# A gated delta layer: smaller tiles in the chunk's inverse, gate weights kept split in memory, and loads asked for at other points

## The chip, the cores and the metric

The kernel runs on one core of a Trainium2 chip. A core has a tensor engine (PE), whose weight loads the profile lists apart as PEld, a vector engine (DVE), a scalar engine (ACT), a general engine (POOL) and an engine that mostly starts transfers (SP); DMA queues move data between the device memory and the on-chip memory. Each engine works through its own row of instructions in order and waits on semaphores where it needs another's result. The metric is the device time of one execution in microseconds (us); less is better. All times below are of the kernel before the change.

## The reference, cut to what matters

One inference step of two layers over 2048 prompt tokens and 32 sample tokens, all in 32-bit floats. The first layer is a gated DeltaNet, the second an attention over a sliding window. The change is in the first layer and in its gate projection and output projection:

```python
proj = x @ w_in                                   # q, k, v, gate z, decays, betas
qkv, new_buf = causal_conv(proj[..., :CONV_DIM], conv_buf, conv_w)
z = proj[..., CONV_DIM:CONV_DIM + A_VW]
...
lower = where(strict, einsum('nbhik,nbhjk->nbhij', k * beta, k) * decay, 0)   # 64 x 64 per chunk and head
tmat = lower + eye(c)
u = triangular_solve(tmat, v * beta)              # needs the inverse of tmat
w = triangular_solve(tmat, k * beta * exp(gcum))
intra = einsum('nbhik,nbhjk->nbhij', q, k) * decay
def step(s, xs):                                  # one chunk after the other
    v_new = ui - wi @ s
    o = qd @ s + ai @ v_new
    s = s * gl + kd.T @ v_new
...
o = o * rsqrt(mean(o * o) + eps) * norm_w * silu(z)
x = layer_norm(alpha * x + o @ w_out)
```

## The kernel before, in words

Every large product is made of three: a 32-bit operand is split into a high part and a rest, and high times high, high times rest and rest times high are summed. Weights come from memory raw (`fetch_weights`), ACT rounds them to `w_hi` (L53), and POOL subtracts that for `w_lo` (L54); `project` then issues 24 products L77, L78 and L79 for a block of 416 tokens, in four steps of six.

The work goes through these stages, one after the other:

1. `P1.qkv`, to about 586 us: the projections of q, k and v, with the convolution on DVE and ACT.
2. The gate's first pass, `P1.z` over the token blocks 0, 1 and 2 for 8 heads, to about 704 us. Each head's 128 columns of weights are fetched and split. A block ends in a tanh on ACT (`zth`, L310), two operations on DVE (L311, L312) and a store by SP (L313). Beside it `Ahead.inverses` makes the small inverses of the first two chunks (`c0`, the 32 sample tokens, and `c1`): a product `g` (L536), a decay `E` (add L516 on DVE, exp L522 on ACT), `npr` = g times E, and a chain of 31 small steps on DVE (L559, L562).
3. The gate's second pass over blocks 3 and 4 for the same 8 heads, which fetches and splits the same weights again. It is not run by itself: `first`, a `Filler`, hands out its steps of six products at fixed places of the next stage.
4. `Delta.run`, the loop over 17 chunks (`i` = 0 is the sample chunk, then 16 of 128 tokens) from about 761 us, one turn taking some 24 to 29 us. The order of its instructions on PE, DVE and ACT is the order in which the code issues them (`manual_schedule`); SP's and POOL's order is left to a scheduler. One turn works on four chunks at once: it inverts the triangular matrix of chunk i+1, makes `g` and `E` of later ones, carries the state `Sp` of chunk i on, and scales its output. The inverse of a chunk and 8 heads has two levels. POOL (and DVE for the last rows) does 31 steps of elimination on 32 x 32 blocks (`chain`); DVE transposes the result into `tcp` (L628, L629). Then `invert` puts the blocks together by products, with the results copied out between them:
   - y1 = the 32 x 32 blocks below the diagonal (products L652, copied out by ACT at L654),
   - `tp` (L658) and `up` (L665), 64 x 64 products with `u32`, which ACT has made of `tcp` by two scaled copies (L634); ACT copies `tp` at L660 and half of `up` at L666, DVE the other half at L667,
   - y2 (L671), copied by ACT at L672, and the last product u2 (L676), copied by ACT at L677 into `u`, with which `vp` (L697) is made.
   Between them stand products that have nothing to do with the inverse: `gq` (L601), `tr` (L572, copied by ACT as `kd`, L575), `vtr` (L586), `op` (L711), and the filler's six at a time.
   The rest of a turn: `npr` (L537) on DVE, `nb` (L541) on ACT, DVE's transpose of it into `L` (L546), the chain's last steps and `tcp` again; `otr` (L771) and `z` (L772) bring out the output.
5. `O1`, the output projection with its layer norm (L1008 to L1013), whose 16 weight tiles `wo` (L955) and two tables are loaded from turn 12 on (`side`), and whose first token tile is fetched and split (`g_hi`, L994, `g_lo`, L995) when its products are due.
6. The second layer, from about 1250 us.

Of the kernel before, what the change touches and what calls it, by code (L numbers as in the profile page):

```python
# [19 lines left out]
D = 1024  # L20
# [142 lines left out]
class P1:  # L163
# [49 lines left out]
    def qkv(self):  # L213
# [32 lines left out]
        for i in range(24):  # L246
# [8 lines left out]
            due += 224 / 22 if i >= 2 else 0  # L255
# [43 lines left out]
    def z(self, blocks, pool, tags, ps, sub, w, wait=False):  # L299

        nc = self.nc
        for h in range(8):
            self.fetched = fetch_weights(nc, self.wp, self.I["w_in"][25 + h]) if h < 7 else None
            self.next, self.sub = None, sub
            for b in blocks:
# [8 lines left out]
                if not wait or b == blocks[-1]:  # L314
                    self.split()
            w = self.next

    def split(self):
        if self.fetched is not None:
            self.next = split_fetched(self.nc, self.wp, self.fetched, self.sub)  # L320
            self.fetched = None

    def first_gate(self, sub):
        return split_weights(self.nc, self.wp, self.I["w_in"][24], sub)
# [123 lines left out]
class Delta:  # L448
# [5 lines left out]
    def __init__(self, tc, es, I, O, T, G):  # L454
# [13 lines left out]
        self.u32 = one.tile([128, 8, 64], F32, tag="u32", name="u32")  # L468
        self.sides = one.tile([128, 2], F32, tag="sides", name="sides")
        for b in range(4):  # L470
            for c in range(2):
                nc.gpsimd.memset(self.sides[32 * b:32 * b + 32, c:c + 1], float(b % 2 == c))
        self.u = one.tile([128, 8, 128], F32, tag="u", name="u")
        nc.gpsimd.memset(self.u[:], 0.0)
        self.y1 = one.tile([128, 8, 64], F32, tag="y1", name="y1")
        nc.gpsimd.memset(self.y1[:], 0.0)
        for hv in (slice(0, 64), slice(64, 128)):
            nc.gpsimd.tensor_copy(self.y1[hv], G["ident"][hv, hv].unsqueeze(1).to_broadcast([64, 8, 64]))
# [142 lines left out]
    def spread(self, ch):  # L621
# [3 lines left out]
        sml = self.sml  # L625
        both = sml.tile([128, 2, 8, 32], F32, tag="ta", name="tcp")
        ch.tcf, ucp = both[:, 0], both[:, 1]
        V.transpose(ch.tcf[:n].rearrange("q p (c d) -> q c d p", d=4), ch.Tt[:n].rearrange("q i c -> q c i"))  # L628
        V.transpose(ucp[:n], ch.tcf[:n])  # L629
        if n == 32:  # L630
            V.tensor_copy(self.u[:32, :, :32], ucp[:32])
            return
        for c in range(2):
            nc.scalar.activation(self.u32[:, :, 32 * c:32 * c + 32], ucp[:], AF.Copy, scale=self.sides[:, c:c + 1])  # L634

    def invert(self, ch):

        nc, V = self.nc, self.nc.vector
        if ch.n == 32:
            return  # L640
        u, sml = self.u, self.sml
        u32, npr = self.u32, ch.npr
        halves = (slice(0, 64), slice(64, 128))

        def new(pool):
# [1225 lines left out]
```

## Time and profile before

| | us |
|---|---|
| median of 3 runs | 2263.8 (2253.85 to 2264.89) |
| the profiled execution | 2252.59 |
| its span | 2250.8 |
| stage 1, `P1.qkv` | to about 586 |
| stages 2 and 3 up to the loop | 586 to about 761 |
| loop `Delta.run` | about 761 to 1190 |
| rest of `O1` | to about 1250 |
| second layer | to the end |

The span runs from the first to the last instruction of the trace; the execution's own time is 1.8 us longer. All times in the text count from the span's start. The trace gives each instruction a start and a duration. A bracket such as `[3.28 <-ACT zth L310]` says that the engine stood idle for 3.28 us before it, and that the last thing it waited for was the tile `zth` that ACT writes at line 310. "PEclk" is the clock granted to PE as a share of the full one.

### The profile page before, as it was taken

The numbers are of one execution on the slowest core, as the hardware profiler recorded it, in microseconds if no ns is written. First come the engines' busy times: TensorE is split into PE (matmuls) and PEld (weight loads), VectorE is DVE, ScalarE is ACT, GpSimd is POOL, SyncE is SP. The second block draws the span as 40 slices with busy tenths as digits, with TensorE's granted clock in tenths as the row PEclk, the third lists the DMA queues.
The fourth block names the chain that finished last, engine by engine and source line by source line (L and its number), as shares of the span: only waits on it lengthen the run. The fifth ranks groups of instructions, "written<-read, shape, count | busy, mean of one in ns | idle before, by whom it ended". The sixth has DMA issues, their size and how long they took to land. (4 is left out here: it accounts for less than half of the span.)

```text
span 2250.8 us, 37045 instructions
## 1 busy us (share of the span) xinstructions
PE 2152.2 (96%) x13370; PEld 1959.0 (87%) x13370; DVE 1470.4 (65%) x2701; ACT 902.7 (40%) x2331; POOL 740.9 (33%) x1193
## 2 busy tenths in 40 slices
PE   8999999999999999999889999899989998999997
PEld 6899999999998889988777787899989986888775
DVE  4798777876484577777655665545844566556662
ACT  4555555444332466656552211311311135444441
POOL 1213111251112387777661210000000024656563
PEclk9999999999999899999999999999999999999999
DMA  7656656567734334435724874888788896233321
GB/s 285 211 185 194 193 179 197 183 193 235 235 117 130 113 117 138 148 114 171 277 75 157 285 224 148 284 279 290 249 297 291 266 286 183 85 104 94 85 80 43
DMA packets 344919, 417.40 MB, mean 185 GB/s; under 512 B 77968, under 2 KB 275696, under 8 KB 344720
## 3 DMA queue, kind: packets, MB, share of 16 engines
q1 hardware_dynamic: 312432, 314.41, 44.1%
q10 hardware_dynamic: 32304, 100.62, 13.4%
q8 instruction: 106, 1.74, 0.3%
q14 instruction: 77, 0.63, 0.1%
HBM read 265.26 MB, written 150.05 MB: 185 GB/s over the span
## 5 line engine op out<-in xcount | busy, mean ns | idle before, releaser
L77 PE MATMUL ps<-act_hi,w_hi 128*128 128x416 f32 x1280 | 459.3, 359 | 6.4 <-ACT R L297 4.3
L79 PE MATMUL ps<-act_hi,w_lo 128*128 128x416 f32 x1280 | 451.7, 354 | 5.2 <-POOL w_lo L54 5.2
L78 PE MATMUL ps<-act_lo,w_hi 128*128 128x416 f32 x1280 | 451.8, 353 | 0.0
L77 PEld LDWEIGHTS ps<-act_hi,w_hi 128*128 128x128 f32 x1280 | 242.4, 189 | 11.2 <-ACT R L297 4.6
L79 PEld LDWEIGHTS ps<-act_hi,w_lo 128*128 128x128 f32 x1280 | 242.7, 190 | 9.7 <-POOL w_lo L54 6.3
L78 PEld LDWEIGHTS ps<-act_lo,w_hi 128*128 128x128 f32 x1280 | 243.2, 190 | 2.7
L54 POOL TENSOR_TENSOR w_lo<-w_raw,w_hi 128x1024 fp32r<-128x1024 f32 x40 | 101.5, 2537 | 381.5 <-ACT w_hi L53 374.9
L1232 PE MATMUL ps<-xs_h,w 128*128 128x416 f32 x560 | 199.4, 356 | 10.9 <-DVE ra L1289 6.9
L1233 PE MATMUL ps<-xs_l,w 128*128 128x416 f32 x560 | 199.9, 357 | 2.9 <-DVE xs_l L1135 2.9
L1234 PE MATMUL ps<-xs_h,w 128*128 128x416 f32 x560 | 198.2, 354 | 0.0
L266 DVE SCALAR_TENSOR_TENSOR y<-R,convw,y 128x2083 f32<-128x2083 f32 x72 | 171.2, 2379 | 24.5 <-ACT y L264 24.4
L559 POOL TENSOR_TENSOR tm<-L,Tt 128x60 f32<-128x60 f32 (+19 forms) x375 | 132.1, 352 | 86.3 <-DVE tm L559 34.1
L562 POOL TENSOR_TENSOR Tt<-Tt,tm 128x60 f32<-128x60 f32 (+19 forms) x375 | 143.4, 382 | 28.5
L1573 POOL TENSOR_TENSOR P<-P,sm 128x384 f32<-128x384 f32 (+2 forms) x128 | 101.0, 810 | 122.5 <-DVE sm L1452 59.1
L1427 POOL MEMSET vd<- 64x768 f32 (+2 forms) x10 | 7.8, 779 | 395.9 <-DVE ra L1289 395.6
L1448 ACT ACTIVATE P<-S,nm 128x192 f32<-128x192 f32 (+2 forms) x260 | 104.8, 419 | 61.4 <-DVE nm L1441 48.9
L1232 PEld LDWEIGHTS ps<-xs_h,w 128*128 128x128 f32 x560 | 106.3, 190 | 13.8 <-DVE ra L1289 7.6
L1289 DVE SCALAR_TENSOR_TENSOR ra<-ps,u 128x416 f32<-128x416 f32 x60 | 35.4, 590 | 122.0 <-PE ps L1234 121.2
L1008 PE MATMUL po<-wo,g_hi 128*128 128x512 f32 (+1 forms) x272 | 110.5, 406 | 3.0 <-DVE r L1013 1.8
L1010 PE MATMUL po<-wo,g_lo 128*128 128x512 f32 (+1 forms) x272 | 107.5, 395 | 4.5 <-DVE g_lo L995 4.5
L1233 PEld LDWEIGHTS ps<-xs_l,w 128*128 128x128 f32 x560 | 106.1, 189 | 5.5 <-DVE xs_l L1135 4.2
L1234 PEld LDWEIGHTS ps<-xs_h,w 128*128 128x128 f32 x560 | 106.9, 191 | 1.2
(292 smaller groups left out, 4808.7 us busy)
## 6 DMA issues: line engine op xcount, KB each, us to landing
w<-s_w ACTq DMA_DIRECT2D x180, 512.0 KB
s_w<-pre_hl SPq DMA_DIRECT2D x160, 256.0 KB
w_raw<-in_w_in SPq DMA_DIRECT2D x40, 512.0 KB
s_wo<-pre_hl SPq DMA_DIRECT2D x64, 256.0 KB
wo<-s_wo SPq DMA_DIRECT2D x32, 512.0 KB
gb<-s_gcum SPq DMA_DIRECT2D x34, 256.0 KB
k<-s_k SPq DMA_DIRECT2D x34, 256.0 KB
s_z<-z SPq DMA_DIRECT2D x40, 208.0 KB
```

The lines of the kernel that those rows point to most:

```text
L77: nc.tensor.matmul(ps, hi[:, k, :], xh[:, k, :], start=(k == 0), stop=False)
L78: nc.tensor.matmul(ps, hi[:, k, :], xl[:, k, :], start=False, stop=False)
L79: nc.tensor.matmul(ps, lo[:, k, :], xh[:, k, :], start=False, stop=(k == KC - 1))
L266: nc.vector.scalar_tensor_tensor(out=y[:], in0=R[:, j:j + W], scalar=self.convw[:, i, j:j + 1], in1=y[:], op0=ALU.mult, op1=ALU.add)
L559: P.tensor_tensor(out=tm[:n, i0 - k:, :w], in0=L[:n, i0:, j:j + 1].to_broadcast(sh), in1=Tt[:n, j:j + 1, :w].to_broadcast(sh), op=ALU.mult)
L562: P.tensor_tensor(out=Tt[:n, i0:, :w], in0=Tt[:n, i0:, :w], in1=tm[:n, i0 - k:, :w], op=ALU.subtract)
L1008: nc.tensor.matmul(ps[:n], ghi[:, k, :n], w[0][k][:, cs], start=(k == 0), stop=False)
L1010: nc.tensor.matmul(ps[:n], glo[:, k, :n], w[0][k][:, cs], start=False, stop=(k == KC - 1))
L1232: nc.tensor.matmul(ps, w[:, 0, k], xh[:], start=first and k == 0, stop=False, skip_group_check=True)
L1233: nc.tensor.matmul(ps, w[:, 0, k], xl[:], start=False, stop=False, skip_group_check=True)
L1234: nc.tensor.matmul(ps, w[:, 1, k], xh[:], start=False, stop=last and k == 3, skip_group_check=True)
L1448: nc.scalar.activation(P[u], src, AF.Exp, bias=nm[:, u:u + 1], scale=1.0, accum_out=sm[:, u:u + 1])
```

## The change

The gate's first pass stores each head's split weights in a new scratch in memory (`wz`, 8 x 2 x 512 KB, by SP), and the second pass reads them back, asked for by ACT's queue, so that L53 and L54 aren't done a second time:

```diff
+    def split_gate(self, sub):
+        w = split_weights(self.nc, self.wp, self.I["w_in"][24], sub)
+        for h in range(8):
+            raw = fetch_weights(self.nc, self.wp, self.I["w_in"][25 + h]) if h < 7 else None
+            yield w
+            for t, d in zip(w, self.T["wz"][h]):
+                self.nc.sync.dma_start(d, t[:].rearrange("p k c -> p (k c)").bitcast(F32))
+            w = split_fetched(self.nc, self.wp, raw, sub) if h < 7 else None
+            yield
+    def kept_gate(self):
+        def load(h):
+            w = [self.wp.tile([128, KC, 128], F32R, tag=t, name=t) for t in ("w_hi", "w_lo")]
+            for t, d in zip(w, self.T["wz"][h]):
+                self.nc.scalar.dma_start(t[:].rearrange("p k c -> p (k c)").bitcast(F32), d)
+            return w
+        w = load(0)
+        yield
+        for h in range(8):
+            ahead = load(h + 1) if h < 7 else None
+            yield w
+            yield
+            w = ahead
```

The inverses made ahead are now issued step by step between steps of the gate's first pass, in PE's order by hand:

```diff
-    Ahead(tc, mid, left, I, O, T, G).inverses(chunks[:2])
-    drain(p1.z((0, 1, 2), zp, ("zth", "z"), p1.ps, nc.gpsimd, p1.first_gate(nc.gpsimd)))
-    w = p1.first_gate(nc.gpsimd)
+    zs = p1.z((0, 1, 2), zp, ("zth", "z"), p1.ps, p1.split_gate(nc.gpsimd))
+    ahead = Ahead(tc, mid, left, I, O, T, G).inverses(chunks[:2])
+    with tc.manual_schedule(engines={mybir.EngineType.PE}):
+        for n in (18, 18, 6, 6, 12, 12):
+            next(ahead)
+            drain(itertools.islice(zs, n))
+        drain(ahead)
+        drain(zs)
+    kept = p1.kept_gate()
+    next(kept)
```

PE's order at that place, before: `g` of the sample chunk stands behind the first block's products (each row is an instruction or a run of alike ones; `act_hi_127` and `act_hi_153` are the blocks 0 and 1).

```order
L78 MATMUL ps<-act_lo_128,w_hi 128x416
L79 MATMUL ps<-act_hi_127,w_lo 128x416
L536 MATMUL g<-k 32x32 x8
L77 MATMUL ps<-act_hi_153,w_hi 128x416
L78 MATMUL ps<-act_lo_154,w_hi 128x416
```

And after: the first half of it stands behind 36 steps, 216 products, of which the last are of block 2 (`act_hi_164`), and the other half six steps further on.

```order
L78 MATMUL ps<-act_lo_165,w_hi 128x416
L79 MATMUL ps<-act_hi_164,w_lo 128x416
L550 MATMUL g<-k 32x32 x4
L77 MATMUL ps<-act_hi_128,w_hi 128x416
L78 MATMUL ps<-act_lo_129,w_hi 128x416
```

So `g` has moved from behind 24 products to behind 216.

In `invert`, `up` is made of 32 x 32 products straight from `tcp` and y1, y2 and u2 are given out in pairs of heads to two halves of the array, and the diagonal blocks are copied:

```diff
-        tp = new(self.pa)
-        for p in range(8):
-            nc.tensor.matmul(tp[:64, p, :], u32[:64, p, :], y1[:64, p, :], start=True, stop=True)
-        ta = sml.tile([128, 8, 64], F32, tag="ta", name="ta")
-        nc.scalar.copy(ta[:64], tp[:64])
+        for b in (0, 1):
+            bs = slice(32 * b, 32 * b + 32)
+            nc.scalar.copy(ta[bs, :, bs], tcf[bs])
         yield
         up = new(self.pb)
-            for hv in halves:
-                nc.tensor.matmul(up[hv, p, :], y1[hv, p, :], u32[hv, p, :], start=True, stop=True)
-        nc.scalar.copy(u[0:64, :, 0:64], up[0:64])
-        V.tensor_copy(u[64:128, :, 64:128], up[64:128])
+            for s, t in pairs:
+                nc.tensor.matmul(up[s, p, 0:32], y1[t, p, :], ucp[t, p, :], start=True, stop=True)
+            nc.tensor.matmul(up[t0, p, 0:32], ucp[t0, p, :], y1[t0, p, :], start=True, stop=True)
+        nc.scalar.copy(ta[t0, :, s0], up[t0, :, 0:32])
+        for s, t in pairs:
+            V.tensor_copy(u[s, :, t], up[s, :, 0:32])
+        V.tensor_copy(self.ub[0:32, :, 32:64], up[64:96, 4:8, 0:32])
+        V.tensor_copy(self.ub[0:32, :, 0:32], ucp[64:96, 4:8])
+        V.tensor_copy(self.ub[32:64, :, 32:64], ucp[96:128, 4:8])
         yield
...
+            for q, dst in ((p, high), (p + 4, low)):
+                nc.tensor.matmul(y2p[dst, q, :], npr[:64, q, 64:128], ta[:64, q, :], start=True, stop=True)
+        nc.scalar.copy(ta[high, 0:4], y2p[high, 0:4])
+        nc.scalar.copy(self.yb[:], y2p[low, 4:8])
+        for b in (2, 3, 0, 1):
+            bs = slice(32 * b, 32 * b + 32)
+            nc.scalar.copy(u[bs, :, bs], ucp[bs])
...
+            nc.tensor.matmul(u2p[low, p, :], ta[high, p, :], u[high, p, high], start=True, stop=True)
+            nc.tensor.matmul(u2q[low, p, :], self.yb[:, p, :], self.ub[:, p, :], start=True, stop=True)
+        nc.scalar.mul(u[low, 0:4, high], u2p[low, 0:4], -1.0)
+        nc.scalar.mul(u[low, 4:8, high], u2q[low, 0:4], -1.0)
```

ACT's order in one turn with filler work, before, from the inverse's first copy to the last exp (`bps` is the product's result, whichever it is; `zth` is the filler's tanh):

```order
L634 ACTIVATE u_6398<-tcp,sides 128x8x32 x2
L654 ACTIVATE y_6410<-bps 32x8x32 x2
L660 COPY ta<-bps 64x512
L575 ACTIVATE kd<-tr,t_ekd 128x128 x4
L666 COPY u<-bps 64x8x64
L610 ACTIVATE gb<-gb 128x512 x2
L672 COPY ta<-bps 64x512
L575 ACTIVATE kd<-tr,t_ekd 128x128 x4
L522 ACTIVATE E<-E,t_ngc 128x128 x4
L310 ACTIVATE zth<-ps 128x416
L677 ACTIVATE u<-bps 64x8x64
L522 ACTIVATE E<-E,t_ngc 128x128 x4
```

The same after; `zth` and the second four of `E` follow the last row.

```order
L662 ACTIVATE y_6423<-bps 32x256 x2
L665 COPY ta<-tcp 32x8x32 x2
L673 COPY ta<-bps 32x8x32
L589 ACTIVATE kd<-tr,t_ekd 128x128 x4
L685 COPY ta<-bps 64x256
L686 COPY yb<-bps 64x256
L689 COPY u<-tcp 32x8x32 x4
L624 ACTIVATE gb<-gb 128x512 x2
L695 ACTIVATE u<-bps 64x4x64
L696 ACTIVATE u<-bps 64x4x64
L589 ACTIVATE kd<-tr,t_ekd 128x128 x4
L536 ACTIVATE E<-E,t_ngc 128x128 x4
```

The copies of u2, one behind `zth` before, are two ahead of the second `kd` now, and four copies of diagonal blocks (L689) have come in ahead of `gb`.

The weights `wo` of `O1` are asked for by ACT's queue, one at each call of `side()`, which comes four times in a turn from turn 11 on; the tables at its twelfth step; and `O1`'s first token tile is fetched at turn 13 and split at turn 14:

```diff
-            if i > 11:
-                side(True)
+            side()
...
+            side()
+            if i in (13, 14):
+                second.step()
...
-            nc.sync.dma_start(w[:, k, s].bitcast(F32), src[k, :, s])
+            queue.dma_start(w[:, k, s].bitcast(F32), src[k, :, s])
...
-        got = self.on.split(self.fetch(*tiles[0]), tiles[0][2])
+        got = self.fetch(*tiles[0])
+        yield 0.0
+        got = self.on.split(got, tiles[0][2])
+        yield 0.0
```

SP's order before, where the first of the 16 loads stand ahead of the loop's own (`gb`, `q`, `k`, `v`, `z` are the chunks' tiles):

```order
L955 DMA wo<-s_wo 128x1024 x4
L773 DMA s_g<-z 128x512
L955 DMA wo<-s_wo 128x1024
L773 DMA s_g<-z 128x512
L503 DMA gb<-s_gcum 128x512 x2
L955 DMA wo<-s_wo 128x1024 x2
L506 DMA q<-s_q 128x512
L955 DMA wo<-s_wo 128x1024 x4
L506 DMA k<-s_k 128x512
L506 DMA v<-s_v 128x512
```

After, they stand in ACT's row, the first two of them here, behind turn 11's copy of `Tt` and between its copies of `o`:

```order
L558 COPY Tt<-tinit 128x256
L977 DMA wo<-s_wo 128x1024
L738 COPY o<-op 128x512
L764 ACTIVATE vn,Xo<-o 128x128 x4
L977 DMA wo<-s_wo 128x1024
```

SP's row has none of the 16 left, and they come four to a turn. Besides, the stage `P1.qkv` hands out the splitting of the second layer's weights at another pace (224/20 from its fifth row on, 224/22 from its third before), and in the loop the filler's steps and the inverse's parts stand in a slightly different order.

More of the change, by code (lines that the diff above doesn't have):

```diff
@@ L254, in qkv @@
                     self.block(R, w, b)
-            due += 224 / 22 if i >= 2 else 0
+            due += 224 / 20 if i >= 4 else 0
             while due >= 1 or i == 23:
@@ L297, in block, with z @@
             self.nc.scalar.copy(R[:, off:off + z - a], ps[:, a:z])
-    def z(self, blocks, pool, tags, ps, sub, w, wait=False):
+    def z(self, blocks, pool, tags, ps, weights):
         nc = self.nc
         for h in range(8):
-            self.fetched = fetch_weights(nc, self.wp, self.I["w_in"][25 + h]) if h < 7 else None
-            self.next, self.sub = None, sub
+            w = next(weights)
             for b in blocks:
@@ L313, in z @@
                 nc.sync.dma_start(self.T["z"][h, :, b * TB:(b + 1) * TB], z[:])
[L314 to L324, printed above, removed]
+                if b == blocks[0]:
+                    next(weights)
+    def split_gate(self, sub):
[20 more added lines that the diff above has]
+            w = ahead
     def left_ps(self):
@@ L668, in invert @@
[L668 to L677 removed]
+            for s, t in pairs:
+                nc.tensor.matmul(up[s, p, 0:32], y1[t, p, :], ucp[t, p, :], start=True, stop=True)
@@ new lines, in invert @@
+        for p in range(4):
+            for q, dst in ((p, high), (p + 4, low)):
[5 more added lines that the diff above has]
+            nc.scalar.copy(u[bs, :, bs], ucp[bs])
+        yield
+        u2p, u2q = new(self.pb), self.pc.tile([128, 8, 64], F32, tag="sc", name="bps")
@@ L1610, in give, with step @@
                 self.done = True
+    def step(self):
+        next(self.gen)
     def rest(self):
@@ L1634, in gated, with side @@
     def gated():
-        yield from p1.z((3, 4), zp, ("zth", "z"), p1.left_ps, nc.gpsimd, w, True)
+        yield from p1.z((3, 4), zp, ("zth", "z"), p1.left_ps, kept)
         left.close()
         o1.append(O1(tc, left, I, O, T, G))
-    def side(o):
-        if o1 and o:
-            drain(itertools.islice(o1[0].on.rest, 2))
-            if o1[0].steps == 5:
+    def side():
+        if o1:
+            next(o1[0].on.rest, None)
+            if o1[0].steps == 12:
                 o1[0].on.tabs = o1[0].on.tables()
             o1[0].steps += 1
-        elif not o1 and not o:
-            p1.split()
     def both(a, b):
```

82 lines of the change are left out of this document (34 added, 48 removed).

## The prediction

> **What bounds the kernel now.** I read the page's list of engines first, then PE's waits, then PE's clock in the windows behind the longest of them, and last the rows of two turns of the loop.
>
> ```profile
> PE 2152.2 (96%) x13370; PEld 1959.0 (87%) x13370; DVE 1470.4 (65%) x2701; ACT 902.7 (40%) x2331; POOL 740.9 (33%) x1193
> ```
>
> PE is busy for 96% of the span, so a gain is either a PE wait that goes, or time at half clock, or PE work that goes while nothing else is due later. The waits of PE between 586 and 1255 us (the columns: total, times, longest):
>
> ```profile
> PE bps L652 <- DVE tcp L628: 8.3, 8, 1.9
> PE vtr L586 <- DMA v<-s_v: 6.2, 1, 6.2
> PE po L1010 <- DVE g_lo L995: 4.5, 1, 4.5
> PE g L536 <- DMA k<-s_k: 4.3, 2, 3.1
> ...
> PE ps L79 <- POOL w_lo L54: 3.9, 2, 2.1
> ...
> PE ps L77 <- ACT w_hi L53: 1.7, 2, 1.0
> PE bps L658 <- ACT y L654: 1.4, 1, 1.4
> ```
>
> Each place the change touches is here. The windows behind those waits (length, busy time of each engine, then granted clock, DMA share, GB/s), and two turns of the loop below them:
>
> ```profile
> 621.70:628.10 6.40, 5.66 (x29) 5.39 (x30) 1.27 (x5) 3.46 (x12) 2.37 (x1) 0.50 0.91 271
> 717.00:723.00 6.00, 4.81 (x16) 4.04 (x17) 0.68 (x1) 0.00 (x0) 1.14 (x1) 0.50 0.79 272
> 737.60:740.80 3.20, 3.20 (x11) 2.99 (x12) 2.48 (x8) 0.58 (x3) 0.00 (x0) 0.50 0.36 112
> 961.00:968.80 7.80, 7.28 (x93) 6.38 (x94) 3.69 (x8) 3.39 (x10) 5.83 (x16) 0.61 0.01 2
> 1078.70:1084.80 6.10, 4.59 (x28) 4.17 (x29) 3.46 (x5) 0.58 (x1) 5.16 (x13) 0.50 1.06 386
> 1167.70:1173.90 6.20, 5.12 (x14) 4.15 (x15) 1.03 (x1) 0.00 (x0) 0.00 (x0) 0.50 0.45 128
> 1187.60:1190.80 3.20, 3.15 (x51) 3.16 (x52) 2.21 (x4) 0.96 (x2) 0.81 (x1) 0.55 0.40 102
> 906.07:932.63 26.56, 26.01 (x274) 24.18 (x273) 21.10 (x46) 16.71 (x52) 22.46 (x52) 1.00 0.49 156
> 1125.67:1149.83 24.16, 21.66 (x248) 20.00 (x248) 19.64 (x44) 16.14 (x51) 19.93 (x52) 1.00 0.29 90
> ```
>
> Every long wait is followed by a stretch at clock 0.50, in which PE's busy time is twice what it would be: such a wait costs itself and half of that busy time.
>
> **The gate's two passes.** At 622 PE waited 3.1 us for `k` and then worked 5.66 us at half clock: 3.1 + 5.66/2 = 5.9. In the new order `g` comes 36 steps later, some 40 us, when `k` has long landed: **5.9 gained**. The chain behind it ends later by the same, which has room as long as it ends before the loop's first turn; below zero only if it does not, 0 to 3 lost. In the second pass the two pairs of waits were 1.0 + 2.1 with 4.81 us at half clock, and 0.7 + 1.8 with 3.20 at half clock (1.7 - 1.0 and 3.9 - 2.1): 5.5 and 4.1. Both are waits for L53 and L54, which are gone there. The second pair I count whole, **4.1**: its weights are asked for a head ahead. In the first pair's place stands a load of 1 MB that ACT asks for only behind the eight exps of the sample chunk:
>
> ```profile
> 709.37 1.81 ACT L522 ACTIVATE E<-E,t_ngc 32x32 f32<-32x32 f32 x8 [4.02 <-DVE E L516]
> 715.41 0.46 PE L77 MATMUL ps<-act_hi,w_hi 128*128 128x416 f32 x1 [0.98 <-ACT w_hi L53]
> ```
>
> The exps ended at 711.2, PE took up the next head's weights at 715.4, and the DMAs behind are 0.79 busy, so I expect the wait to come back nearly as long: **1 gained**, between 3 lost and 5.5 gained. The 16 stores into `wz` (8 MB) lie in the first pass, whose products run without a wait; they would cost something only by delaying `k` or the raw weights, which are a head ahead. The 16 loads sit on ACT's queue, for whose cost see the last part of the loop.
>
> **POOL's share of the loop.** One L54 falls on the end of the chain:
>
> ```profile
> 957.77 0.32 DVE L559 TENSOR_TENSOR tm<-L,Tt 128x8 f32<-128x8 f32 x1
> 958.12 2.29 DVE L562 TENSOR_TENSOR Tt<-Tt,tm 128x8 f32<-128x8 f32 x1
> 958.02 2.36 POOL L54 TENSOR_TENSOR w_lo<-w_raw,w_hi 128x1024 fp32r<-128x1024 f32 x1
> 961.16 0.69 PE L652 MATMUL bps<-tcp,npr 32*32 32x32 f32 x32 [1.93 <-DVE tcp L628]
> ```
>
> DVE's last small step takes 2.29 us while POOL's subtraction runs. PE waits 1.93 for it and then has 7.28 us of work at 0.61 of the clock, of which 39% are lost: 1.9 + 2.8 = **4.7 gained**, since no L54 is left in the loop. The others in the loop fall where DVE's small steps aren't last; they may give up to 2.5 more, or nothing.
>
> **The inverse in a turn with filler work.** Here are a turn's rows on ACT, DVE and PE, in this order:
>
> ```profile
> 914.30 1.14 ACT L575 ACTIVATE kd<-tr,t_ekd 128x128 f32<-128x128 f32 x4 [0.94 <-PE tr L572]
> 915.31 1.28 ACT L522 ACTIVATE E<-E,t_ngc 128x128 f32<-128x128 f32 x4
> 916.48 0.52 ACT L310 ACTIVATE zth<-ps 128x416 f32<-128x416 f32 x1
> 917.04 0.65 DVE L311 TENSOR_SCALAR z<-ps,nwh 128x416 f32<-128x416 f32 x1 [3.28 <-ACT zth L310]
> 931.78 0.72 DVE L628 STREAM_TRANSPOSE tcp<-Tt 128x256 f32<-128x256 f32 x1
> 920.07 0.60 PE L771 MATMUL otr<-ident,o 128*128 128x128 f32 x4
> ```
>
> From 917.04, when `zth` lets it go, DVE has no gap until it has made `tcp` at 932.5, and PE's next turn starts at 932.63. So two things bound this turn together: PE, 26.01 busy of 26.56, and the way y1 (906.07), second `kd`, `E`, `zth`, DVE, `tcp`. The change shortens the one and lengthens the other. The rows for it:
>
> ```profile
> L665 PE MATMUL bps<-u,y 64*64 64x64 f32 x32 | 1.1, 221 | 0.0
> L671 PE MATMUL bps<-ta,npr 64*64 64x64 f32 x16 | 1.1, 221 | 0.0
> L654 ACT ACTIVATE y<-bps 32x256 f32<-32x256 f32 x2 | 0.8, 376 | 0.1
> L541 ACT COPY nb<-npr 32x256 f32<-32x256 f32 x4 | 1.6, 404 | 1.7 <-DVE npr L537 1.6
> L672 ACT COPY ta<-bps 64x512 f32<-64x512 f32 x1 | 0.6, 581 | 0.0
> ```
>
> PE: 32 products on two corners of the array take the 1.1 us that 16 on one corner take, 34 against 69 ns each. So y2 and u2 in pairs would take 0.55 each instead of 1.1, `tp` (1.1) goes, and `up` with 48 small products I put at its old 1.1: 2.2 us less in a turn. ACT: a copy of 32 x 256 takes 0.40 whatever it reads, and 64 x 256 no row shows; it lies between that 0.40 and the 0.58 of 64 x 512, and I take 0.40. From y1's result ACT now does y1 0.8, `ta` 0.8, a corner of `up` 0.4, `kd` 1.1, y2 0.8, diagonal blocks 1.6, `gb` 1.2, u2 0.8, and then the second `kd`: 7.5 us, with waits for `up` (1.1 us behind y1, and for `gq` ahead of it) and for y2, which must wait until DVE has copied `up` out of the same buffer. Laid out: y1's products end at 906.8, its copies at 907.5, `ta` 908.3; `up` runs 908.1 to 909.2; the corner 909.6; `kd` 910.9; DVE's three copies end near 910.7, y2 near 911.3; its copies 912.1, the blocks 913.7, `gb` 914.9, u2 915.7; the second `kd` starts there instead of at 914.30. That is 1.4 later; with DVE's copies at the 0.65 of its step at 917.04 it is 2.1, and 0.7 if copies between on-chip tiles take half. **I take 1.5**, and what follows on DVE moves along with it, while PE's saved time turns into idle time ahead of y2 and `otr` (which at 920.07 follows DVE's `o` at once). Ten turns with filler work: **15 lost**, 7 to 21.
>
> **A turn without filler work** (four of them) has 24.16 us and these rows:
>
> ```profile
> 1136.34 0.69 DVE L537 TENSOR_TENSOR npr<-g,E 128x512 f32<-128x512 f32 x1 [0.74 <-ACT E L522]
> 1139.40 1.64 ACT L541 COPY nb<-npr 32x256 f32<-32x256 f32 x4
> 1142.23 2.00 DVE L546 STREAM_TRANSPOSE L<-nb 128x1024 f32<-128x1024 f32 x1
> 1144.40 0.26 POOL L559 TENSOR_TENSOR tm<-L,Tt 128x31 f32<-128x31 f32 x1 [0.47 <-DVE tm L559]
> 1651.36 0.33 ACTq L1214 DMA_DIRECT2D w<-s_w  x1
> ```
>
> `nb` was ready at 1141.0, 1.2 us before DVE took it up, so of the 1.5 only some 0.3 comes through; POOL's chain, which waits 0.47 in the whole turn, leaves as little room for a gain. The `wo` loads cost ACT 0.33 each by the row of another load, two of the four ahead of `E`: 0.9 in a turn, **3.6 lost**, 0 to 6. The last chunk's inverse, with nothing beside it, had a wait of 1.4 and 3.15 us at half clock; its stages now wait for ACT in the same way: **1 lost**, 2 gained to 2 lost.
>
> **The output projection's loads.** SP asked for most of the 8 MB in this window, and `v` came 6.2 us late:
>
> ```profile
> 1056.00:1084.00 28.00, 18.60 (x199) 16.59 (x199) 19.51 (x44) 12.22 (x38) 21.32 (x56) 0.91 1.00 363
> ```
>
> The wait and the half clock behind it make 6.2 + 4.59/2 = **8.5 gained**, since the same bytes are now spread over four turns with 90 GB/s of their own traffic. The first tile's `g_lo`, 4.5 + 5.12/2 = **7.1 gained**, as it is split a turn earlier; what is late next there is the inverse of the last chunk, counted above. If the split on ACT and DVE only pushes the loop's own work, 4 of it remain.
>
> **Sum:** 5.9 + 1 + 4.1 + 4.7 + 8.5 + 7.1 = 31.3 gained; 15 + 3.6 + 1 = 19.6 lost; **11.7 us faster**: 2252.6 becomes 2240.9. The median of the runs shown is 11.2 above the profiled execution, two of three runs near 2264 and one at 2254; I add half of that and predict **2246.5**.
>
> **Rivals.** *The small tiles pay.* If the copies take half of what I think, or if PE is the bound of a turn, its 2.2 us come through: between a loop that comes out even (31.3 gained) and ten turns shorter by 2.2 (53.3), so 2199 to 2221, middle 2210. For it: PE is 98% busy in such a turn. Against it: DVE's gapless stretch, which doesn't depend on PE's speed. [...]
>
> *The stalls only change places.* The change then doesn't do what it says: `wz` and `wo` asked for by an ACT that is itself behind arrive late, and half of the 31.3 stays: 15.6 against 19.6, 4 slower, or with a loop that loses 8 less, 4 faster. About 2253 on the profiled execution's scale, 2258 on mine. For it: ACT now both waits for PE and asks for the loads.
>
> *Half clock in every turn.* PE's idle time of a filler turn grows from 0.55 to some 4 us. In the rows a wait of 1.4 (at 1187) was already followed by 0.55 of the clock, and one of 1.93 cost 2.8 us more. My layout has the idle time in pieces of 0.7 and 1.1; if they fall together before `otr` in one piece over 1.4, each of ten turns loses 2.8: 28 lost, minus 11.7: 16 **slower**, 2269 on the first scale, 2274 on mine. Against it: four waits of 0.2 to 0.9 in each turn without filler leave the clock at 1.00. [...]
>
> **How the numbers follow.** Chances: forecast 0.50, small tiles pay 0.21, stalls change places 0.18, half clock 0.11. A difference of 0.5%, 11.3 us, is about what a measurement of this kernel can tell from no change. My forecast's 11.7 lies on that line, with 7 to 21 for the loop and the loads' bounds around it, so a little more than half of it counts as faster, 0.28, and 0.22 as the same. With 0.21 and 0.02 from the two rivals: faster 0.51; same 0.22 + 0.14 + 0.02 = 0.38; slower 0.02 + 0.09 = 0.11. The range leaves out the full pay of the tiles and the half clock's worst: 2212 to 2266.
>
> **What would show it.** Right: no wait before `g` near 640, none for `w_hi` or `w_lo` beyond the first head's, none over 1 us for `v` or `g_lo`; turns with filler of 28 us in which DVE's `z` follows `zth` as now; turns without of 25. Wrong: filler turns under 26 us (the tiles pay), a clock below 0.9 in them (the third rival), or PE waits on `wz` and `wo` loads. A shift of `P1.qkv` by its new pace would upset everything; its products run without a gap now, and I give it nothing.

## The result, and the profile after

| | before | after |
|---|---|---|
| median of 4 runs each | 2260.19 us (2253.85 to 2264.89) | 2229.72 us (2226.38 to 2234.94) |
| the profiled execution | 2252.59 us | 2230.72 us |
| its span | 2250.8 us | 2228.9 us |

The ratio of the two is 0.9879 [0.9851, 0.9908]: the changed kernel is faster by 1.2%, 30.5 us by the medians and 21.9 by the profiled executions. The forecast was 11.7 on the profiled scale. The direction was right, the time lies in the range, and nearly twice as much was gained as forecast.

I cut both spans at two marks that each trace has: the first `y1` of the loop and the last one (L652 before, L660 after).

| | before | after | difference |
|---|---|---|---|
| start to the last `zth` of the first pass | 704.83 | 707.99 | +3.2 |
| from there to the first `y1` | 69.09 | 55.36 | -13.7 |
| first turn of the loop | 24.42 | 24.47 | 0 |
| ten turns with filler work | 270.55 | 269.24 | -1.3 |
| three turns without | 80.94 | 75.74 | -5.2 |
| the fourth, with the first output tile | 35.74 | 28.59 | -7.15 |
| last `y1` to the end | 1065.2 | 1067.5 | +2.3 |

The page's line of PE after the change has 41 us less of busy time, and the span is shorter by only 22. Part of the busy time was half clock (the mean granted clock of the span is 0.979 before and 0.983 after), and part of what went has come back as idle time:

```profile
PE 2111.1 (95%) x13370; PEld 1919.0 (86%) x13370; DVE 1479.8 (66%) x2765; ACT 909.8 (41%) x2403; POOL 718.5 (32%) x1176
```

PE's waits of the changed kernel between 586 and 1235 us (total, times, longest):

```profile
PE bps L684 <- DVE ub L676: 18.3, 16, 1.8
PE bps L660 <- DVE tcp L641: 6.5, 7, 1.0
PE g L550 <- ACT kd L589: 5.9, 9, 1.4
PE ps L77 <- DVE z L310: 5.8, 1, 5.8
PE gq L615 <- DVE vn L601: 4.3, 14, 0.4
...
PE po L1030 <- DVE r L1035: 3.1, 3, 2.6
PE ks L705 <- DVE Sp L754: 3.1, 4, 0.9
PE vtr L600 <- DMA v<-s_v: 2.7, 1, 2.7
...
PE ps L79 <- DMA w_lo<-s_wz: 0.9, 1, 0.9
```

The waits for ACT's `w_hi`, POOL's `w_lo` and for `g_lo` are gone; one of 0.9 for the load of `w_lo` stands in their place, and that for `v` has shrunk from 6.2 to 2.7. Two are new: 1.1 us ahead of y2 in each turn (16 times, L684), and one of 5.8 us in the first pass.

**The way up to the loop.** The stretch from the last `zth` to the first `y1`, first of the kernel before (length, busy time of PE, PEld, DVE, ACT, POOL, granted clock, DMA share, GB/s):

```profile
704.83:773.92 69.09, 62.24 (x371) 55.34 (x369) 33.68 (x61) 26.43 (x81) 17.04 (x35) 0.85 0.44 133
```

and of the changed one:

```profile
707.99:763.35 55.36, 53.02 (x370) 48.38 (x368) 30.97 (x60) 22.81 (x76) 8.07 (x26) 1.00 0.63 206
```

PE has the same number of matmul records, 371 and 370. Its idle time falls from 6.85 to 2.34 us, and its busy time by 9.2 because the clock is 1.00 instead of 0.85: 4.5 + 9.2 = 13.7.

**The new wait of the first pass**, in the changed kernel's timelines of PE, DVE and SP's queue:

```profile
629.49 0.71 PE L77 MATMUL ps<-act_hi,w_hi 128*128 128x416 f32 x1 [5.80 <-DVE z L310]
...
628.78 1.21 DVE L310 TENSOR_SCALAR z<-ps,nwh 128x416 f32<-128x416 f32 x2 [6.70 <-DMA s_z<-z]
...
613.77 0.45 SPq L323 DMA_DIRECT2D s_wz<-w_lo  x1
...
616.07 1.17 SPq L517 DMA_DIRECT2D gb<-s_gcum  x2
617.28 1.26 SPq L520 DMA_DIRECT2D k<-s_k  x2
618.59 1.68 SPq L517 DMA_DIRECT2D gb<-s_gcum  x2
620.32 1.13 SPq L520 DMA_DIRECT2D k<-s_k  x2
621.54 0.93 SPq L938 DMA_DIRECT2D Sp<-in_state_delta  x2
622.58 0.94 SPq L312 DMA_DIRECT2D s_z<-z  x2
```

It is read from the bottom up. SP issued in this order: the store of a split weight, then without a gap the loads of the first chunks (`nm`, `tinit`, `gb`, `k`, `Sp`), and only at 622.58 the store of `z`. Before the change it stood ahead of the loads of `gb` and `k`:

```profile
613.47 1.14 SPq L313 DMA_DIRECT2D s_z<-z  x2
```

The tile `z` has two buffers, both waiting to be stored; DVE waits 6.70 us for one of them, so PE's accumulator isn't emptied and PE waits 5.80. Half clock follows in this trace: 0.73 granted between 630 and 640 us.

**The loop.** Windows of five turns of the changed kernel, two with filler work, then the three kinds without:

```profile
842.04:870.64 28.60, 27.30 (x272) 25.49 (x272) 22.49 (x50) 17.72 (x57) 18.71 (x50) 0.82 0.38 115
...
1004.05:1030.65 26.60, 24.11 (x274) 22.04 (x273) 21.49 (x50) 17.43 (x57) 19.40 (x51) 1.00 0.43 130
...
1057.06:1084.22 27.16, 20.86 (x248) 19.06 (x248) 20.40 (x48) 17.24 (x56) 19.18 (x52) 0.94 0.81 264
1108.54:1132.80 24.26, 19.35 (x248) 17.69 (x248) 20.61 (x48) 17.02 (x56) 19.67 (x52) 1.00 0.67 213
1132.80:1161.39 28.59, 24.29 (x257) 21.08 (x257) 18.09 (x45) 14.70 (x45) 15.60 (x37) 1.00 0.33 105
```

In the turn at 1004.05 PE's work is 24.11 us instead of 26.01 in the turn that the prediction showed, and the turn is as long as before, 26.60: PE's 1.9 us have become waits. The turn at 842.04 has the same work at a clock of 0.82. In the middle of the turn at 1004.05, on ACT, DVE and PE:

```profile
1008.55 0.68 PE L684 MATMUL bps<-ta,npr 64*64 64x64 f32 x16 [1.16 <-DVE ub L676]
1009.27 0.37 ACT L685 COPY ta<-bps 64x256 f32<-64x256 f32 x1 [0.70 <-PE bps L684]
1010.02 1.66 ACT L689 COPY u<-tcp 32x256 f32<-32x256 f32 x4
1013.29 1.11 ACT L589 ACTIVATE kd<-tr,t_ekd 128x128 f32<-128x128 f32 x4
...
1016.00 0.65 DVE L310 TENSOR_SCALAR z<-ps,nwh 128x416 f32<-128x416 f32 x1 [4.11 <-ACT zth L309]
```

The second `kd` comes 9.24 us behind `y1` (1004.05), before it was 8.23 (914.30 less 906.07): 1.0 later. The 1.66 us of diagonal copies stand on the way to it.

### The profile page after: what moved, and what is told of

It reads as the page before. It is cut to its first block, busy times and chain, and to the rows that moved or that the text cites. A ratio compares the mean times of both kernels' runs of the same rounds, so it can differ in the third digit from the quotient of the medians.

```text
span 2228.9 us, 37186 instructions
## 1 busy us (share of the span) xinstructions
PE 2111.1 (95%) x13370; PEld 1919.0 (86%) x13370; DVE 1479.8 (66%) x2765; ACT 909.8 (41%) x2403; POOL 718.5 (32%) x1176
## 4 chain that ended last, share of the span: by engine, by line
PE 71%; DVE 13%; DMA 6%; ACT 5%; issue 3%; SPq 2%; POOL 1%; ACTq 0%; DVEq 0%; POOLq 0%
PE ps L77 8%; PE ps L79 8%; PE ps L78 8%; PE ps L1257 5%; PE ps L1258 5%; PE ps L1259 5%; PE ot L1611 3%; PE po L1498 3%; PE po L1499 3%; PE po L1500 3%; PE S L1590 2%; PE po L1030 2%; PE po L1032 2%; PE po L1031 2%; PE tr L1605 2%
## 5 line engine op out<-in xcount | busy, mean ns | idle before, releaser
L77 PE MATMUL ps<-act_hi,w_hi 128*128 128x416 f32 x1280 | 459.4, 359 | 10.0 <-DVE z L310 5.8
L79 PE MATMUL ps<-act_hi,w_lo 128*128 128x416 f32 x1280 | 450.4, 353 | 2.1 <-POOL w_lo L54 1.2
L77 PEld LDWEIGHTS ps<-act_hi,w_hi 128*128 128x128 f32 x1280 | 242.3, 189 | 14.5 <-DVE z L310 6.1
L79 PEld LDWEIGHTS ps<-act_hi,w_lo 128*128 128x128 f32 x1280 | 242.3, 189 | 6.3 <-POOL w_lo L54 1.7
L54 POOL TENSOR_TENSOR w_lo<-w_raw,w_hi 128x1024 fp32r<-128x1024 f32 x32 | 83.9, 2622 | 343.0 <-ACT w_hi L53 342.9
```

The costliest lines, as they stand in the source:

```text
L77: nc.tensor.matmul(ps, hi[:, k, :], xh[:, k, :], start=(k == 0), stop=False)
L79: nc.tensor.matmul(ps, lo[:, k, :], xh[:, k, :], start=False, stop=(k == KC - 1))
```

## The experiments

Eleven kernels, in three groups, each with runs of the kernel before on its own chip: its medians were 2260.43, 2262.98 and 2257.03. Ratios are against it.

### The inverse as it was, and the diagonal copies moved

The first run leaves all of the change but gives `invert` its old products and copies back, and its parts their old places in the turn:

```diff
-        for b in (0, 1):
-            bs = slice(32 * b, 32 * b + 32)
-            nc.scalar.copy(ta[bs, :, bs], tcf[bs])
+        for p in range(8):
+            nc.tensor.matmul(tp[:64, p, :], u32[:64, p, :], y1[:64, p, :], start=True, stop=True)
```

> The changed kernel with the inverse of before (tp, up, y2, u2 in 64 x 64, u32 by two scaled copies, its parts at their old places in the turn); all else as changed. By the prediction's step (the new inverse lengthens each of ten turns with filler work by 1.5 us and each without by 0.9) this is some 15 to 19 us faster than the changed kernel, near 2212. By the theory that the two bounds of a turn nearly cancel (ACT's second kd 1.0 us later, PE's work 1.9 us shorter) it is within 4 us of the changed kernel's 2230, with turns with filler of 26.3 to 26.6 and PE busy 26.0 in them. If the small tiles pay by themselves it is 5 to 20 us slower than the changed kernel.

Measured: 2232.35 us, 0.9869 [0.9849, 0.989]. A turn with filler work of this kernel:

```profile
895.64:922.22 26.58, 25.94 (x273) 24.17 (x272) 20.72 (x46) 16.65 (x52) 20.16 (x51) 1.00 0.40 132
```

The ten turns take 265.6 us here and 269.2 in the changed kernel. So the new inverse loses 3.6 there, not 15, and the kernels' medians cannot be told apart. (In its trace half clock falls into the three turns without filler work (from 1062.40 and 1082.88), which take 82.5 us instead of 75.7; the comparison therefore rests on the ten turns and not on the whole.) The difference has two halves. The changed kernel's turns 2 and 3 of the ten have half clock (28.20 and 28.60 us, at a clock of 0.88 and 0.82); in the kernel with four buffers for `z`, below, the same two took 26.07 and 24.96 and the ten 264.9. The first four turns gain in the kernel with four buffers (103.3 there, with one stretch of half clock, 107.8 here) and the last six lose: 27.15, 27.36, 27.39, 26.63, 26.60 and 26.41 in the changed kernel against 26.58, 26.52, 26.51, 26.43, 26.29 and 25.48, together 3.7.

The second run moves ACT's copies of the diagonal blocks to places where ACT has time: one beside y1, two beside `up`, so that only one is left between y2 and the second `kd`:

```diff
+        nc.scalar.copy(u[0:32, :, 0:32], ucp[0:32])
         yield
...
+        for b in (2, 3):
+            bs = slice(32 * b, 32 * b + 32)
+            nc.scalar.copy(u[bs, :, bs], ucp[bs])
+        yield
...
-        for b in (2, 3, 0, 1):
-            bs = slice(32 * b, 32 * b + 32)
-            nc.scalar.copy(u[bs, :, bs], ucp[bs])
+        nc.scalar.copy(u[32:64, :, 32:64], ucp[32:64])
...
-            go(v, r, r, r, g, r, r, v, r, k, r, d)
+            go(v, r, r, r, g, r, r, v, r, k, v, r, d)
```

> The changed kernel with the four copies of diagonal blocks (1.66 us on ACT ahead of gb) moved into gaps that ACT has earlier: one behind the copies of ta, two behind the first kd, one left in place. If ACT's way to the second kd, E and zth sets a turn's length, the second kd starts near 8.2 us into the turn instead of 9.2, and the ten turns with filler shorten by 0.7 to 1.0 each: 7 to 10 us faster than the changed kernel. If PE's work or DVE's own row bounds the turn, the second kd is earlier by the same and the turns stay within 0.3: under 3 us.

Measured: 2224.52 us, 0.9832 [0.9809, 0.9855].

```profile
924.08:950.22 26.14, 23.86 (x274) 21.96 (x273) 21.65 (x50) 17.56 (x57) 20.47 (x52) 1.00 0.53 172
```

The second `kd` is back at 8.1 us behind `y1`. Of the last six turns the first three take 26.1 to 26.4 us instead of 27.2 to 27.4, and the last two 25.43 and 25.33 instead of 26.60 and 26.41; the one between, 26.76 against 26.63, has half clock here (eight products of `op` take 1.92 us at 982.21 and 1.06 elsewhere) and a clock of 1.00 there. So in these turns ACT's way to the second `kd` sets the pace, as the prediction had it; PE's work is nearly the same in both, 23.9 and 24.1 us. The first four turns don't move with ACT: `zth` comes 1.1 us earlier in them, and they take 25.96, 24.90 and 24.85 us where the clock was full, as with four buffers for `z` (25.92 and 24.96).

### Why PE waits 5.8 us in the first pass

Two kernels attack the wait from two sides: `z` of the first pass stored by POOL's queue, which has no stores of weights in it, and four buffers for `z` instead of two.

```diff
-                nc.sync.dma_start(self.T["z"][h, :, b * TB:(b + 1) * TB], z[:])
+                queue = nc.gpsimd if b < 3 else nc.sync
+                queue.dma_start(self.T["z"][h, :, b * TB:(b + 1) * TB], z[:])
```

> The changed kernel with the z stores of the gate's first pass issued by POOL's queue instead of SP's; the same bytes at the same place in the program. By the theory that SP's row made the stores late (they stand behind the loads of gb, k and the state, issued at 622 although z was ready at 612), PE's wait of 5.8 us near 629 and the half clock behind it go: 7 to 9 us faster before the loop. By the rival that the DMAs are simply full there (share 1.0 with the 1 MB a head of wz stores), the wait stays within 2 us of 5.8, or moves to g's load of k.

```diff
-    zp = new_pool(tc, left, "p1_z", 2, side="left")
+    zp = new_pool(tc, left, "p1_z", 4, side="left")
```

> The changed kernel with four instead of two buffers for zth and z. If PE's wait near 629 is for z's buffer, whose store is late, two more buffers carry DVE over the 10 us: the wait of 5.8 and the half clock behind it go, 7 to 9 us faster before the loop. If the loads of gb and k are what is late, PE waits at g instead, 3 to 6 us, and little is gained.

Measured: 2227.99 us, 0.9849 [0.9829, 0.9869], and 2223.8 us, 0.9834 [0.9818, 0.985]. In both the wait is gone and the clock between 620 and 640 us is 1.00, with the DMAs still 0.87 and 0.84 busy. PE's waits up to 760 us with POOL's queue, where little else is left:

```profile
PE ps L77 <- DMA w_hi<-s_wz: 2.1, 1, 2.1
PE ps L79 <- DMA w_lo<-s_wz: 1.6, 1, 1.6
```

and with four buffers:

```profile
PE ps L77 <- DMA w_hi<-s_wz: 2.9, 1, 2.9
PE ps L79 <- DMA w_lo<-s_wz: 1.9, 1, 1.9
```

So the cause is SP's order and the two buffers. The last `zth` of the first pass comes at 697.95 and 698.86, some 10 us earlier than in the changed kernel. And the wait hid another: PE now comes sooner to the second pass, and the kept weights of its second head, which the prediction had expected to be late, are late. The first `y1` was at 763.35 in the changed kernel; it comes at 757.53 with POOL's queue, and at 763.70 with four buffers, where half clock (0.66 in 710 to 720 us) followed the two waits and came once more from 753.47 to 760.30, without a wait; the last section comes back to that stretch.

### The loads of the output weights, the first output tile and the kept weights, each undone

```diff
-        self.rest = load_out_weights(nc, self.one, wo, nc.scalar)
+        self.rest = load_out_weights(nc, self.one, wo, nc.sync)
```

> The changed kernel with the 16 loads of wo in the loop issued by SP again, at the changed spacing (one at each side call). By the theory that the spacing is what counts (8 MB over four turns), little changes: PE's longest wait for v stays under 3.5 us, within 4 us of the changed kernel's 2230. By the rival that SP's scheduled row moves them ahead of the chunks' own loads as it did before, the wait for v comes back to 5 to 6 us with half clock behind it, 5 to 9 us slower than the changed kernel.

Measured: 2237.18 us, 0.9895 [0.9858, 0.9933]. PE's wait for `v` is back, and its turn takes 30.94 us instead of 27.16:

```profile
PE vtr L600 <- DMA v<-s_v: 6.3, 1, 6.3
```

The code asks for the loads at the same calls in both kernels, but SP's order is the scheduler's: SP issued all 16 between 1039.59 and 1067.64 us, many of them ahead of the chunks' own loads, and ACT from 1047.25 to 1141.05, where the order is by hand. So it is ACT's queue that keeps the loads apart; whether `v` would come in time if ACT asked for them in one bunch was not tried. The time of the whole, 2237.18, cannot be told from the changed kernel's.

```diff
-            if i in (13, 14):
-                second.step()
```

> The changed kernel without the two early steps of the output projection, so that its first token tile is fetched and split when its products are due, as before. By the prediction's step the wait for g_lo (4.5 us before) and the half clock behind it come back in the last turns: 4 to 7 us slower than the changed kernel, the turn behind the 15th chunk's inverse near 35 us instead of 28.6. If the loop's last turns gave the gain for another reason, it stays at 28.6.

Measured: 2234.24 us, 0.9886 [0.9855, 0.9918]. Here too the old wait is back, and the turn has 35.46 us instead of 28.59, 6.9 more, though the times of the whole again cannot be told apart:

```profile
PE po L1030 <- DVE g_lo L1015: 5.2, 1, 5.2
```

The third of them splits the gate's weights a second time, as before, and stores none:

```diff
-            for t, d in zip(w, self.T["wz"][h]):
-                self.nc.sync.dma_start(d, t[:].rearrange("p k c -> p (k c)").bitcast(F32))
...
-    def kept_gate(self):
+    def kept_gate(self, sub):
+        w = split_weights(self.nc, self.wp, self.I["w_in"][24], sub)
```

> The changed kernel without wz: no stores in the first pass, and the second pass fetches the weights raw and splits them again on ACT and POOL (L53, L54). By the prediction's terms for this part (4.1 and 1 ahead of the loop, 4.7 in it) it is some 10 us slower than the changed kernel, less what the stores cost the first pass: if the wait of 5.8 near 629 is of the stores' making it goes here, and the balance is 0 to 3 slower; if it is not, it stays and the balance is 8 to 12 slower. One turn of the loop has DVE's step at 2.3 us beside an L54 again.

Measured: 2230.6 us, 0.9875 [0.9837, 0.9914]: no difference from the changed kernel that these runs can tell. Its trace has no wait of 5.8 us, and SP stores `z` at 614.23, ahead of the loads of `gb` and `k` again; so the order that made the wait came with the stores of `wz`. Two turns with POOL's subtraction in them are 29.60 and 30.64 long, 2.4 and 3.3 more than in the changed kernel. It does not meet the end of the chain there but another operation of DVE, which takes 2.88 us instead of 0.68, and PE waits for what DVE does behind it:

```profile
905.37 2.36 POOL L54 TENSOR_TENSOR w_lo<-w_raw,w_hi 128x1024 fp32r<-128x1024 f32 x1
905.41 2.88 DVE L624 TENSOR_TENSOR k<-k,gb 128x512 f32<-128x512 f32 x1
909.54 2.05 PE L740 MATMUL sp<-vs,kd 128*128 128x128 f32 x16 [2.30 <-DVE z L783]
```

Part of the 2.4 is a stretch of half clock from 894.65 on, which stands ahead of the subtraction and has nothing to do with it. Another wait has grown, that of `g` for `k` (1.1 in the changed kernel):

```profile
PE g L542 <- DMA k<-s_k: 3.2, 1, 3.2
```

Keeping the weights pays in the loop and costs in the first pass; its sum could not be told from nothing as long as `z` is stored behind those loads.

### Parts together, and the changed kernel again

The diagonal copies moved, and `z` stored by POOL's queue:

> The changed kernel with the diagonal copies moved early and the z stores of the first pass by POOL, both as in the runs above: if the two gains add, PE's wait near 629 is gone, the turns with filler work take 24.9 to 26.4 us, and it is 9 to 14 us faster than the changed kernel, 2216 to 2221.

Measured: 2223.0 us, 0.9828 [0.9789, 0.9866]. That is short of the 2216 to 2221 expected if the two gains add, but their sum, a ratio of some 0.980, lies within the interval, so that the time does not decide it. In its trace five of the turns with filler work have half clock where the kernel with the moved copies alone had it in one of these, as in this one against the 26.14 us of the same turn there:

```profile
912.47:939.95 27.48, 25.36 (x274) 23.38 (x273) 21.44 (x50) 17.80 (x57) 19.90 (x52) 0.94 0.52 162
```

The code of the loop is the same in both; the turns only start at other times. The last section comes back to it.

The changed kernel was then run once more, in one group with two others:

> The changed kernel once more, beside the next two on one chip: within 5 us of its 2230. If the half clock stretch in the third and fourth turn with filler work (28.2 and 28.6 us against 24.9 for the one behind them) belongs to the order of the work, it is there again in the same turns; if it hangs on when a turn starts, other turns have it.

Measured: 2235.06 us, 0.9899 [0.9871, 0.9926]. In its trace other turns have half clock: the second and third of the ten, whose windows at first had 0.88 and 0.82, now read 0.94 both, and so do the first, the fifth and the ninth:

```profile
784.94:812.39 27.45, 24.79 (x273) 23.52 (x273) 21.70 (x50) 17.83 (x57) 19.68 (x52) 0.94 0.39 124
...
891.21:918.65 27.44, 25.39 (x274) 23.50 (x273) 21.32 (x50) 17.78 (x57) 19.12 (x51) 0.94 0.44 140
```

The next asks for the kept weights of the second head together with the first's, ahead of the second pass:

```diff
-        w = load(0)
+        ahead = [load(0), load(1)]
```

> The changed kernel with the second head's kept weights asked for at once with the first's, ahead of the sample chunk's exps instead of behind them. If those loads are late because ACT asks for them behind the exps, PE no longer waits for w_hi or w_lo near 715 (0.9 us in the changed kernel, 2 to 5 us and half clock where the first pass was shorter): 1 to 3 us faster than the changed kernel. If the DMAs are full there whoever asks, the wait stays, or the loads of the first chunks' k and q get later instead.

Measured: 2231.1 us, 0.9886 [0.9858, 0.9914], 4 us less than the changed kernel beside it, within what these runs can tell from nothing. The wait for `w_lo` is gone; the one for `z` is there and sets the pace ahead of it:

```profile
PE ps L77 <- DVE z L310: 6.9, 2, 5.8
```

Last, three parts together: the moved copies, four buffers for `z`, and the early load.

> The early diagonal copies, four buffers for zth and z and the early second load together, all as in the runs above. If the gains add it is 10 to 16 us faster than the changed kernel, 2214 to 2220. By the rival that a faster start only moves turns onto other half clock stretches or the output projection's loads (a wait of 5 to 7 us for its residual tile near 1217, where the loop ended 9 us earlier), it is 2221 to 2226, like each of them alone.

Measured: **2213.7 us** (2208.81 to 2218.56), 0.9798 [0.9768, 0.9829]: the fastest of all, 21.4 us less than the changed kernel in the same group. PE's waits up to 760 us are down to this:

```profile
PE g L550 <- DMA k<-s_k: 1.2, 1, 1.2
PE ps L77 <- DVE z L310: 0.7, 1, 0.7
```

With neither `z` nor the kept weights late, the first `y1` is at 756.26, and the ten turns take 260.0 us. No kernel had the moved copies and the four buffers without the early load, so its share in this was not measured.

## Why the prediction was right in direction and short in size

**The step that failed** is "Ten turns with filler work: **15 lost**, 7 to 21". With the 4.7 of L54 the prediction had these turns 10.3 longer; they are 1.3 shorter. The single pieces were nearly right: the second `kd` comes 1.0 later (1.5 in the prediction), the copy of 64 x 256 takes 0.37 (0.40), y2 takes 0.68 (0.55). What was wrong is that one turn's picture was laid over all ten. In the first four `zth` stands ahead of the last product, not behind the second `kd`, and the run with moved copies shows that ACT's way doesn't set their length. There PE's shorter work comes through in part: 103.3 against 107.8 us, where its busy time fell by 2.5 us a turn. That PE's own row sets their length is argued from this. In the other six the 1.0 is there and the run with moved copies shows that ACT is the reason, but only 0.6 us a turn, 3.7 in all, remain; in the eighth and ninth turn, for one, the old inverse left DVE idle for 0.6 us more behind `zth`, and that room took it up. So the inverse costs 3.6 us in the loop by one trace of the changed kernel, and about nothing by that with four buffers (264.9 against 265.6): the rival "the small tiles pay" was true of four turns, the forecast of six.

**The first pass: 5.9 gained** is wrong in sign. The wait for `k` went, and a wait of 5.8 us for the store of `z` took its place. The prediction counted the stores as free beside PE's work ("they would cost something only by delaying `k` or the raw weights"). It looked at what the stores carry, not at how SP's order would change with them: the store of `z` fell behind the loads of the first chunks. The last `zth` comes 3.2 later instead of 5.9 earlier. The pass itself is 5.3 longer, since its first `zth` came 2.1 earlier, at 607.50 instead of 609.64; whether that is the new pace of `P1.qkv`, which the prediction gave nothing, no run separates.

**The second pass: 1 + 4.1** became 13.7. The first pair of waits did not come back, apart from 0.9 for `w_lo`. The reason was shown by taking the 5.8 us away: PE arrived too late to need the weights any earlier. So 5.5 less 0.9 came from this pair and 4.1 from the other, and the rest, some 5.1, was not in the sum: before the change 10.24 us at half clock began at 761.28, while PE had no gap (5.00 busy of 5.00 us at 0.63, then at 0.50), and the changed kernel's trace has no such stretch. I count that as luck and not as the change's doing: the stretch stands in four of the twelve traces of changed kernels too (from 760.29 with the moved copies, 753.47 with four buffers, 751.29 without `wz`, 745.56 with the three parts), and the last section has the starts of the products that stand ahead of it. By chance the misses of the two passes nearly cancel: 11.0 predicted for both, 10.6 measured.

**L54 in the loop, 4.7:** the turn at whose end it fell and the one behind, which had the half clock, took 28.54 and 29.37 us, 4.9 more than the turns on both sides (26.56 and 26.46); in the changed kernel they take what their neighbours do, 27.35 and 27.39. The term was right. The run that brought the subtractions back does not test it, since they fell at another place of the turn; it shows only that one beside DVE made PE wait 2.1 to 2.3 us there too.

**The output projection's loads, 8.5, and 3.6 for their issue:** the three turns are 5.2 shorter, where 8.5 less three quarters of 3.6 is 5.8. Both terms were too large: 2.7 us of the wait remain and 3.4 us at half clock, and a turn without it is 24.26 where it was 24.16 (24.28 and 24.30 in the kernel whose loads SP issued), so that the loads on ACT's queue cost 0.1 a turn at most and not 0.9.

**The first tile, 7.1:** the turn is 7.15 shorter, and 6.9 came back when the split was put off. Right.

**The last chunk's inverse, 1 lost:** PE waits 1.80 us ahead of y2, 6.8 us at half clock follow from 1164.40, and the second `otr` behind it stands 15.76 us behind the last `y1` instead of 15.39: 0.4 lost. Another 1.9 are lost behind that, of which the largest piece seen is a wait for `r` in the output projection, 2.55 us where one of 1.81 stood. In the second trace of the changed kernel that wait is 6.8 us, so this part differs by more from one execution to the next than by the change.

**The median.** The profiled execution of before, 2252.59, was below the lowest of its other runs; that of the changed kernel, 2230.72, is near its median. I added 5.6 for this. The medians stand 7.6 and -1.0 from their profiled executions.

**The rivals.** The stalls did change places in the first pass, and nowhere else to that extent. The half clock came, in two of ten turns of one trace and five of the other, not in all; one stretch of 3.4 us at half clock cost 1.2 to 1.4 us, the difference of the same turns in the kernel with moved copies and the one with both parts. The prediction's "every long wait is followed by a stretch at clock 0.50" holds for the windows that it shows and not for all waits of that trace: PE waited 1.81 us for `r` up to 1246.33, and the clock is 1.00 from there to 1260. Nor is PE's busy time quite "twice what it would be" there: the products L77 to L79 behind the wait for `k` start 0.35 us apart at clock 0.50 (623.95 to 627.77) and 0.19 apart behind it (628.34 to 629.29).

## What to carry to other kernels

Before a store is called free, list its queue's order anew, which a scheduler may change with it, and ask whose buffers wait for what comes later. When a cost is worked out in one turn of a loop, look at the others for the place of the same instructions in their rows: where the order differs, another engine may set the length. A wait that is taken away can uncover the next late transfer: the kept weights were 1.6 to 2.9 us late only once `z` was not (0.9 in the changed kernel), and the early load alone, with the wait for `z` still ahead of it, could not be told from nothing. A gain read from one trace should be looked for in others of the same code: 5.1 us of the gain here are a stretch at half clock that stands in the trace of the kernel before and in four of the twelve of changed kernels.

## What the runs showed of the hardware that was not expected

The stretches at half clock that were read last one, two or three times 3.413 us and start whole multiples of it apart. In the changed kernel they start between 760 and 1170 us at 768.454, 816.240, 843.547, 1065.413 and 1164.400 and last 3.413, 6.827, 10.240, 3.413 and 6.827; divided by 3.413 us, the length of the shortest, the distances from the first start are 14.0, 22.0, 87.0 and 116.0. In the kernel before they start between 730 and 1190 us at 737.388, 761.282, 962.668, 1078.721, 1167.468 and 1187.948 and last 3.413, 10.240, 6.827, 6.827, 6.827 and 3.413; there the distances are 7.0, 66.0, 100.0, 126.0 and 132.0. A period is here a stretch of 3.413 us, laid end to end with the others through one such start.

Two pairs of periods of the kernel with both parts, each time the one that holds the wait ahead of y2 and the one behind it:

```profile
887.05:890.46 3.41, 2.25 (x72) 1.93 (x73) 2.95 (x8) 3.10 (x10) 3.10 (x7) 1.00 0.02 5
890.46:893.87 3.41, 3.41 (x29) 3.07 (x27) 1.31 (x3) 2.41 (x7) 2.85 (x8) 0.50 0.29 85
...
1023.58:1026.99 3.41, 2.25 (x50) 1.93 (x40) 2.72 (x8) 3.06 (x10) 3.17 (x6) 1.00 0.00 0
1026.99:1030.41 3.42, 2.88 (x36) 2.50 (x34) 1.90 (x3) 3.38 (x11) 2.87 (x8) 1.00 0.53 157
```

Both periods have the same wait of 1.16 us and the same 2.25 us of busy time, and only the first is followed by clock 0.50:

```profile
889.42 0.68 PE L690 MATMUL bps<-ta,npr 64*64 64x64 f32 x16 [1.16 <-DVE ub L678]
...
1025.55 0.68 PE L690 MATMUL bps<-ta,npr 64*64 64x64 f32 x16 [1.16 <-DVE ub L678]
```

The wait starts 1.21 us behind the start of the period in the first case and 0.81 in the second. With periods laid in each of the eleven traces of kernels with the new inverse, all 18 such waits in the ten turns (1.16 to 1.23 us long) that start 1.14 to 1.71 us into a period were followed by half clock, and none of the 84 that start up to 0.81 or from 1.83 on.

PE's busy time in a period and its number of matmul records do not tell whether half clock follows. The first line is of the kernel before, ahead of the stretch at 761.28: PE is busy for 3.41 of 3.41 us, and half clock follows. The second is of the second trace of the changed kernel, with the same 2.25 us and as many records as at 887.05, and the clock stays full behind it:

```profile
757.87:761.28 3.41, 3.41 (x27) 2.91 (x26) 1.70 (x1) 3.32 (x12) 0.00 (x0) 1.00 0.50 154
...
920.17:923.58 3.41, 2.25 (x72) 1.88 (x72) 2.95 (x9) 2.31 (x7) 3.10 (x7) 1.00 0.02 5
```

Nearly all the products of the first are those of the sample chunk on 32 rows, `op` and `sp`:

```profile
758.64 1.06 PE L715 MATMUL op<-vs,at 32*32 32x128 f32 x8
759.63 2.30 PE L729 MATMUL sp<-vs,kd 32*128 32x128 f32 x16
```

In the five of thirteen traces in which these two start at the edge of a period or up to 0.77 us behind it, half clock follows; in the eight in which they start 0.84 to 2.36 us behind it, none does. What makes the clock fall was not shown.

A turn of 27.48 us is 8 times 3.413 and 0.17 more, so that the wait of the next turn starts nearly where this one's stood in its period; the starts of the five turns with half clock in the kernel with both parts go 1.21, 1.38, 1.66, 1.71 and 1.28 us. After a turn of 26.33 us it starts a full us earlier. I take this for the reason that five turns in a row have it, and that the same code has it elsewhere in the next trace; no run tested it.
